# PSUM banks of the decay products, the pool products and the last merge in a two-block transformer kernel

## The chip, the core and the metric

The kernel runs on one core of a Trainium2 chip. Time is device time in microseconds (us) from one launch, which computes everything. TensorE (PE in the rows; PEld is its weight load) does the matrix products and writes them to PSUM, eight banks of 128 partitions x 512 float32. VectorE (DVE) and ScalarE (ACT) read PSUM and work in SBUF; GpSimd (POOL) works in SBUF alone; SyncE (SP) issues the transfers. The order of each engine's instructions is fixed when the program is built; an instruction waits for others by semaphores.

## What is computed

A sequence of 512 tokens of width 1024 goes through two blocks. The first is stick-breaking attention, cross-attention to a memory and a convolutional feed-forward part, each with a layer norm. The change lies in the second block, which takes the normed sequence through one wide projection into three branches and merges them:

```python
w = -softplus(-(w0 + tanh(wd) @ w_up)) - 0.5        # branch a: decay
a = sigmoid(a0 + ad @ a_up)                          #           rate
y_a = rwkv7(r, exp(-exp(w)), k, v, a, ...) * silu(z) # 8 heads of 64, a state carried over 512 steps
y_b = b * conv3(c * u) * silu(z)                     # branch b
pooled[g] = mean over the last 2, 4, 8, 16 tokens of u - u       # branch c
y_c = (einsum('bsgc,gcd->bsgd', pooled, pool_w) * pool_scale) * silu(z)
proj = einsum('nbsc,ncd->nbsd', stack([y_a, y_b, y_c]), w_branch)
merged = sum over n of sigmoid(p_gate[n]) * proj[n]
x = x + rms_norm(merged @ w_out, post_norm_w)
```

## The kernel before

Every large product is done in three passes of single-pass float32 matmuls. Each operand is split into a rounded part and a remainder (`wh`, `wl` for weights; names ending in `h` and `l` for activations), and high x high, high x low and low x high are summed in one bank (`mm3`, L214). The split costs a ScalarE cast and a VectorE subtraction for each weight tile (L144, L145) and each activation tile (L236 and L237, or L1461 and L1462). Activations are kept transposed, with channels on partitions, so a product fills one bank of 128 x 512.

A stream of foreground code issues the projections one after the other: `chunk` takes a bank, runs 24 matmuls into it and hands it to whoever reads it. Background work is written as Python generators that yield a number of ticks; after each 1550 ns of matmul time, by the program's own count, `tick` advances each of them and puts its instructions behind those already issued. That sets the order by hand: nothing is reordered later, and a matmul that waits holds up all that stand behind it on TensorE.

PSUM is given out by `bank`, in four groups of equal tiles, of which each is a ring:

```python
def bank(tag, name, shape=None):
    return psp.tile(shape or [P, S], F32, tag=tag, bufs={"g": 3, "a": 2, "b": 2, "c": 1}[tag], name=name)
```

A product that takes a bank waits until the last reader of the product that had it before is done. Group "g" is used by the projections (`ps_chunk`), the merges (`ps_br`) and the last projection (`ps_rows`); "b" by most small products of the recurrence; "a" by its masked products `ps_ac`, by `ps_w` and by `ps_y`.

The recurrence of branch a runs in the background, for two pairs of heads at a time (`rwkv_pair`). For a pair p it issues: two decay products `ps_wa` (L1040), whose sigmoids `sg` and `ai` ScalarE reads out; the running sum `cs` (VectorE, L1045); the norms `ps_ss` with `ss` and a chain of small VectorE instructions (L1051, L274 to L285), and ScalarE's `rb`; the products `ps_ri` and `ps_rk` (L1066, L1078), the second of which VectorE reads into `bv` (L1080); transposes `ps_tok` (L1098); the masked products `ps_ac` in two halves (L1111), which VectorE reads with L1115 into `aa` and `arr`; then more `ps_tok`, which ScalarE copies into `at` and `kbt` (L1127, L1133).

Meanwhile the foreground issues the projections of branch c. `pool_window` builds the means on GpSimd and VectorE and splits them into `plh` (ScalarE) and `pll` (GpSimd); `pool_mix` multiplies them by `pool_w` into `ps_mix` (three matmuls), which VectorE reads at L1372. The last `merge` (n = 0) makes eight products `ps_br` of 12 matmuls. VectorE multiplies each by its gate (L1401), GpSimd adds it to `merged` (L1402), and `fin`, two products later, splits the sum into `mgh` (ScalarE) and `mgl` (VectorE, L1462). The last projection then reads these in `ps_rows`; its weights are split in the same stretch, the last of them by the L145 that stands at 1312 us.

Of the kernel before, what the change touches and what calls it, by code (L numbers as in the profile page):

```python
# [14 lines left out]
ALU = mybir.AluOpType  # L15
# [53 lines left out]
def model_kernel(ctx: ExitStack, tc: tile.TileContext, a: dict, out: bass.AP, dbg: dict):  # L69
    nc = tc.nc  # L70
    stop = dbg.get("stop")
    V, G, A, T = nc.vector, nc.gpsimd, nc.scalar, nc.tensor
# [14 lines left out]
    def bank(tag, name, shape=None):  # L87
        return psp.tile(shape or [P, S], F32, tag=tag, bufs={"g": 3, "a": 2, "b": 2, "c": 1}[tag], name=name)

    def bigt(name, shape, dt=F32R):  # L90
        return big.tile(shape, dt, tag="B", bufs=5, name=name)
# [4 lines left out]
    def sub(s, *idx):  # L96
        return Split(s.hi[idx], s.lo[idx])
# [52 lines left out]
    def w_take():  # L150
        i = taken[0]
        taken[0] += 1
        while i not in ready:
            w_load()
            if not w_conv():
                assert i in ready, "no room for the weights"
        return ready.pop(i)

    def w_done(n=1):
        freed[0] += n  # L160
# [60 lines left out]
    def mm3(ps, pairs, start=True, stop=True, ticks=True):  # L221

        n = len(pairs)
        for z in range(3):
            for j, (l, r) in enumerate(pairs):
                due = mm(ps, (l.hi, l.hi, l.lo)[z], (r.hi, r.lo, r.hi)[z], start=start and z == 0 and j == 0,
                         stop=stop and z == 2 and j == n - 1)
                if due and ticks:
                    tick()
# [15 lines left out]
    def chunk(x, n=S, tag="g"):  # L245
        ps = bank(tag, "ps_chunk")
        gemm_T(ps[:, 0:n], w_take(), x, 0, n)
        w_done()
        return ps
# [42 lines left out]
    def col(name, j=0, n=1):  # L292
        o = COLS[name] + j
        return colp[:, o:o + n]
# [309 lines left out]
    for c in range(KC):  # L604
        ps = chunk(memT, M)
# [144 lines left out]
    for n in range(2):  # L750
# [8 lines left out]
        for m in range(2):  # L759
            d = (ALLS, m, slice(n * 512, (n + 1) * 512))  # L760
# [56 lines left out]
    for c in range(KC):  # L817
        ps = chunk(hT)
# [71 lines left out]
    for pi, (f0, f1) in enumerate(parts):  # L890
        if pi:
            run_ahead(spare_in(bigt("wxh", [P, 8, 512]), bigt("wxl", [P, 8, 512])))
        for f in range(f0, f1):
# [4 lines left out]
            for isv in range(2):  # L898
                ps = lead.pop(0)() if lead else chunk(hT)
# [79 lines left out]
    def temp(name, shape=None, dt=F32):  # L979
        return b2.tile(shape or [P, S], dt, tag="e", bufs=6, name=name)  # L980
# [52 lines left out]
    def rwkv_pair(p, ab, abd, a21):  # L1033
# [2 lines left out]
        q = p % NB2  # L1036
        sg, ai = slot("sg"), slot("ai")
        for z, (o, b) in enumerate(((sg, "w0"), (ai, "a0"))):
            ps = bank("b", "ps_wa")
            T.matmul(ps, wup[hrow(z), tok(p)], wa[hrow(z)], start=True, stop=True)  # L1040
            A.activation(o, ps, AF.Sigmoid, bias=col(b, p))
        sq = slot("sq")
# [4 lines left out]
        ps = bank("b", "ps_ss")  # L1047
# [16 lines left out]
        ps = bank("b", "ps_ri")  # L1064
# [11 lines left out]
        ps = bank("b", "ps_rk")  # L1076
# [18 lines left out]
        def tokens(src):  # L1095
            ps = bank("b", "ps_tok", [P, 4, P])
            for t in range(NT):
                T.transpose(ps[:, t], src[:, tok(t)], ident)  # L1098
            return ps

        ps = tokens(v)
# [28 lines left out]
        for h in range(2):  # L1130
            ps = tokens(kbh.rearrange("p t z i -> p (t z i)")[:, 512 * h:512 * h + 512])
# [3 lines left out]
        ps = bank("c", "ps_av", [P, NT, 2, CH])  # L1135
# [178 lines left out]
    def y_split(i, x):  # L1314
        yield wait["ysp"]
        split_to(x, ycur["t"][:, 0, i], ycur["t"][:, 1, i], V)
        ysplit.add(i)
# [48 lines left out]
    def pool_mix(i, pw, pooled, zs):  # L1366
        while not pooled:
            yield
        yield wait["mx"]
        ps = bank("b", "ps_mix")  # L1370
        mm3(ps, [(sub(pw, ALLS, i), pooled["h"])], ticks=False)
        V.scalar_tensor_tensor(zs, ps, col("pool_scale", i), zs, ALU.mult, ALU.mult)  # L1372
        yield from y_split(i, zs)

    def gate(g):
        A.activation(g, proj_in(), AF.Sigmoid)
        return g

    def merge(n):
        if "t" not in mT:  # L1380
            mT["t"] = bigt("merged", [P, KC, S], F32)
        merged = mT["t"]
        y = [sub(Split(ycur["t"][:, 0], ycur["t"][:, 1]), ALLS, i) for i in range(4)] if n else ya
        ahead_g = [gate(temp("gate"))] if n else []
        for d in range(KC):
            if n and d < KC - 1:
                ahead_g.append(gate(temp("gate")))
            g = ahead_g.pop(0) if n else gates[:, d]
            if d % 2 == 0:
                w = w_take()  # L1390
            wv = Split(*[x.rearrange("p (c k n) -> p c k n", c=2, k=4) for x in (w.hi, w.lo)])
            if n:
                until(lambda: len(ysplit) == 4)
            ps = bank("g", "ps_br")
            mm3(ps, [(sub(wv, ALLS, d % 2, k), y[k]) for k in range(4)])
            if d % 2:
                w_done()
            if n == 1:
                V.tensor_tensor(merged[:, d], ps, g, ALU.mult)
            else:  # L1400
                V.tensor_tensor(g, ps, g, ALU.mult)  # L1401
                (V if n else G).tensor_tensor(merged[:, d], merged[:, d], g, ALU.add)  # L1402
            if n == 0 and d > 1:
                fin(d - 2)
        if n == 0:
            fin(KC - 2)
            fin(KC - 1)
# [3 lines left out]
    ps = proj_in()  # L1411
# [166 lines left out]
```

## Time and profile before

| | us |
|---|---|
| median of three runs | 1358.63 (1357.41 to 1358.8) |
| the profiled execution | 1359.82 |
| its span, first to last instruction | 1358.1 |
| TensorE busy | 1328.8 |
| VectorE busy | 827.8 |
| ScalarE busy | 527.9 |
| GpSimd busy | 257.4 |

The mean granted clock of TensorE over the span is 0.993. A row of the timeline gives the start, the time to the end of the last of its instructions, engine, line, operation, output and inputs, shape and count, and in brackets how long the engine was idle before it and what ended that. Matmuls overlap, so a row's time is a little longer than the distance to the next start. Where the clock is halved, matmuls take twice as long.

### The profile page before, as it was taken

The page shows a single profiled execution, that of the slowest core. Times are in us where ns is not written, and L with a number is a line of the kernel's source. Part 1 is how long each engine was busy: PE and PEld are TensorE (multiplying, and loading weights), DVE is VectorE, ACT ScalarE, POOL GpSimd, SP SyncE. Part 2 cuts the span into 40 slices and gives each one's busy share as a digit, 9 for nine tenths or more (in the row PEclk, how much of TensorE's full clock was granted, in tenths as well). Part 3 has the DMA queues.
Part 4 walks back from the last instruction along what each step waited for, and adds up shares of the span by engine and source line. Part 5 has one row for each costly group of instructions (what it writes and reads, how often), then busy time and mean ns, then how long its engine had stood idle before and what let it go on. Part 6 is the DMA issues. An engine that isn't in the chain of part 4 may idle for free.

```text
span 1358.1 us, 19442 instructions
## 1 busy us (share of the span) xinstructions
PE 1328.8 (98%) x7804; PEld 1112.2 (82%) x7804; DVE 827.8 (61%) x1425; ACT 527.9 (39%) x780; POOL 257.4 (19%) x244
## 2 busy tenths in 40 slices
PE   8999999999999999999999999999999989999997
PEld 7988888788879888888888888888878768887876
DVE  5787887765577555522556866666335567743575
ACT  6565665144423444321344235532323434222330
POOL 1333432000000434400132211200001342000230
PEclk9999999999999999999999999999999899999999
DMA  5121343242223333233234113234221223422331
GB/s 190 63 90 55 105 148 125 85 148 94 82 74 125 111 94 106 93 103 98 94 124 161 50 57 106 77 107 109 78 79 62 70 76 92 114 89 78 117 132 63
DMA packets 54666, 133.25 MB, mean 98 GB/s; under 512 B 19632, under 2 KB 21552, under 8 KB 54576
## 3 DMA queue, kind: packets, MB, share of 16 engines
q1 hardware_dynamic: 54576, 132.01, 30.7%
q8 instruction: 61, 1.00, 0.3%
q14 instruction: 29, 0.24, 0.1%
HBM read 126.48 MB, written 5.24 MB: 97 GB/s over the span
## 4 chain that ended last, share of the span: by engine, by line
PE 83%; DVE 10%; ACT 3%; DMA 2%; issue 1%; POOL 0%; DVEq 0%; SPq 0%; ACTq 0%; POOLq 0%
PE ps_chunk L214 48%; PE ps_rows L214 9%; PE ps_d L214 6%; PE ps_br L214 3%; PE ps_v L214 3%; PE ps_lead L214 3%; DVE wl L145 2%; PE ps_s L488 1%; PE ps_o L542 1%; ACT wh L144 1%; DVE lnt L650 1%; PE ps_t L510 1%; PE ps_z L214 1%; PE ps_o L214 1%; DMA wr<-in_w_xq_dram 1%
## 5 line engine op out<-in xcount | busy, mean ns | idle before, releaser
L145 DVE TENSOR_TENSOR wl<-wr,wh 128x1024 fp32r<-128x1024 f32 x196 | 251.8, 1286 | 144.5 <-ACT wh L144 143.9
L144 ACT CAST wh<-wr 128x1024 fp32r<-128x1024 f32 x196 | 204.9, 1046 | 116.9 <-PE ps_d L214 51.2
L214 PE MATMUL ps_chunk<-h3Th,wh 128*128 128x512 f32 x480 | 126.0, 398 | 0.0
L214 PE MATMUL ps_chunk<-h3Tl,wh 128*128 128x512 f32 x480 | 125.8, 397 | 0.0
L214 PE MATMUL ps_chunk<-h3Th,wl 128*128 128x512 f32 x480 | 124.3, 395 | 0.0
L872 DVE SCALAR_TENSOR_TENSOR c<-ps_chunk,colp,c 128x511 f32<-128x511 f32 x80 | 59.9, 749 | 92.2 <-ACT c L870 90.7
L878 POOL TENSOR_TENSOR c<-c 128x512 f32<-128x512 f32 x21 | 42.5, 2023 | 357.9 <-ACT c L877 209.3
L214 PEld LDWEIGHTS ps_chunk<-h3Th,wh 128*128 128x128 f32 x480 | 90.0, 190 | 21.1 <-issue 2.3
L214 PEld LDWEIGHTS ps_chunk<-h3Tl,wh 128*128 128x128 f32 x480 | 90.0, 190 | 19.8 <-issue 0.8
L214 PEld LDWEIGHTS ps_chunk<-h3Th,wl 128*128 128x128 f32 x480 | 89.6, 189 | 18.9
L214 PE MATMUL ps_chunk<-h2Th,wh 128*128 128x512 f32 x320 | 79.0, 389 | 0.0
L214 PE MATMUL ps_chunk<-h2Tl,wh 128*128 128x512 f32 x320 | 79.0, 389 | 0.0
L214 PE MATMUL ps_chunk<-h2Th,wl 128*128 128x512 f32 x320 | 79.0, 389 | 0.0
L500 POOL TENSOR_TENSOR w<-r 128x511 f32<-128x511 f32 x40 | 58.7, 1468 | 85.4 <-DVE r L498 76.7
L870 ACT ACTIVATE c<-ps_chunk,colp 128x512 f32<-128x512 f32 x40 | 31.1, 779 | 109.7 <-PE ps_chunk L214 109.7
L214 PEld LDWEIGHTS ps_chunk<-h2Th,wl 128*128 128x128 f32 x320 | 60.1, 188 | 12.5
L214 PEld LDWEIGHTS ps_chunk<-h2Tl,wh 128*128 128x128 f32 x320 | 60.1, 188 | 12.5
L214 PEld LDWEIGHTS ps_chunk<-h2Th,wh 128*128 128x128 f32 x320 | 60.0, 188 | 12.4
L498 DVE TENSOR_TENSOR_SCAN r<-keep,masks 128x512 f32<-128x512 f32 x40 | 59.8, 1509 | 12.5 <-ACT keep L496 8.0
L214 PE MATMUL ps_chunk<-xTh,wh 128*128 128x512 f32 x128 | 35.6, 402 | 5.3 <-ACT xTh L376 5.3
L214 PE MATMUL ps_d<-wh,gvb 128*128 128x512 f32 x128 | 39.7, 389 | 0.0
L496 ACT ACTIVATE keep<-ps_s 128x512 f32<-128x512 f32 (+1 forms) x48 | 24.5, 526 | 37.8 <-PE ps_s L488 37.7
(396 smaller groups left out, 2623.6 us busy)
## 6 DMA issues: line engine op xcount, KB each, us to landing
wr<-in_w_in_dram SPq DMA_DIRECT2D x65, 512.0 KB, 3.6
wr<-in_w_ff_dram SPq DMA_DIRECT2D x44, 512.0 KB, 3.6
wr<-in_w_dn_dram SPq DMA_DIRECT2D x22, 512.0 KB, 3.5
wr<-in_w_qk_dram SPq DMA_DIRECT2D x14, 512.0 KB, 3.5
wr<-in_w_br_dram SPq DMA_DIRECT2D x12, 512.0 KB, 3.5
wr<-in_w_v_dram SPq DMA_DIRECT2D x8, 512.0 KB, 3.7
wr<-in_w_xk_dram SPq DMA_DIRECT2D x8, 512.0 KB, 4.0
wr<-in_w_o_dram SPq DMA_DIRECT2D x8, 512.0 KB, 3.5
```

Source lines behind the costliest of these rows:

```text
L144: A.copy(w.hi, raw)
L145: lo_of.tensor_tensor(w.lo, raw, f32(w.hi), ALU.subtract)
L214: T.matmul(ps, l, r, start=start, stop=stop)
L488: T.matmul(ps[:, o:o + n], q[e][:, tok(i)], part[:, 0:n], start=z == 0 and o == 0, stop=z == 1 and i == parts[-1][1])
L496: A.activation(keep[:, j * n:(j + 1) * n], ps[:, 0:n], AF.Sigmoid, scale=-0.125)
L498: V.tensor_tensor_scan(r[:, ::-1], keep[:, ::-1], masks[:, m, ::-1], 1.0, ALU.mult, ALU.max)
L500: G.tensor_tensor(t[:, 0:S - 1], r[:, 1:S], r[:, 0:S - 1], ALU.subtract)
L510: T.transpose(ps[:, n], src[:, o + j * P:o + (j + 1) * P], ident)
L542: T.matmul(ps[:, j * P:S], lhs, part, start=(j == 0 and z == 0), stop=j == 2 and z == 1)
L870: A.activation(c, ps, AF.Identity, scale=cw(2), bias=col("ffb", j))
L872: V.scalar_tensor_tensor(c[:, 2 - r:S], ps[:, 0:S - 2 + r], cw(r), c[:, 2 - r:S], ALU.mult, ALU.add)
L878: (V if end else G).tensor_tensor(cv, cg, cv, ALU.mult)
```

## The change

It gives three kinds of products other groups of banks, and moves three sums to another engine. The decay products `ps_wa` of pairs 1, 2 and 3 take a bank of group "a"; pair 0 stays on "b". The pool products `ps_mix` take a bank of "g". In the last merge the eight products take their banks from "g", "a" and "b" in turn, so that all seven banks of these groups are used. The sums of its last three products (d = 5, 6, 7) are done by VectorE. Nothing is computed differently.

```diff
@@ rwkv_pair
-            ps = bank("b", "ps_wa")
+            ps = bank("a" if p else "b", "ps_wa")
             T.matmul(ps, wup[hrow(z), tok(p)], wa[hrow(z)], start=True, stop=True)
@@ pool_mix
-        ps = bank("b", "ps_mix")
+        ps = bank("g", "ps_mix")
@@ merge
-            ps = bank("g", "ps_br")
+            ps = bank("g" if n else "gab"[d % 3], "ps_br")
...
-                (V if n else G).tensor_tensor(merged[:, d], merged[:, d], g, ALU.add)
+                (V if n or d > 4 else G).tensor_tensor(merged[:, d], merged[:, d], g, ALU.add)
```

TensorE's instructions stand in the same order as before; what changes is what they wait for. The first place is on TensorE at pair 3's decay products. In brackets stands whose semaphore an instruction waits for (the engine's name).

```order
 L1078 MATMUL ps_rk<-rkh,bd1r 128x512 [waits PE_49,Activation_49]
 L1078 MATMUL ps_rk<-rkl,bd1r 128x512 [waits DVE_49]
-L1040 MATMUL ps_wa<-wa,wup 128x512 [waits PE_49]
-L1040 MATMUL ps_wa<-wa,wup 128x512 [waits DVE_49]
+L1040 MATMUL ps_wa<-wa,wup 128x512 x2
 L214 MATMUL ps_chunk<-h3Th,wh 128x512 x5
 L214 MATMUL ps_chunk<-h3Tl,wh 128x512 x8
 L214 MATMUL ps_chunk<-h3Th,wl 128x512 x3
-L1049 MATMUL ps_ss<-bd_81,sq 128x2 [waits Activation_49]
+L1049 MATMUL ps_ss<-bd_81,sq 128x2 [waits PE_49,Activation_49]
```

The second decay product no longer waits for VectorE; `ps_ss` waits for ScalarE as before.

The second place is on TensorE behind the first pool product, where the transposes `ps_tok` of the scaled keys `kbh` stand between chunk matmuls.

```order
 L214 MATMUL ps_mix<-plh,pw 128x512
 L214 MATMUL ps_chunk<-h3Th,wl 128x512 x5
+L1098 MATMUL ps_tok<-ident,kbh 128x128 [waits Activation_49]
+L1098 MATMUL ps_tok<-ident,kbh 128x128 x3
+L214 MATMUL ps_chunk<-h3Th,wh 128x512 [waits DVE_49]
+L214 MATMUL ps_chunk<-h3Th,wh 128x512 x7
+L214 MATMUL ps_chunk<-h3Tl,wh 128x512 x8
 L1098 MATMUL ps_tok<-ident,kbh 128x128 [waits DVE_49]
 L1098 MATMUL ps_tok<-ident,kbh 128x128 x3
-L214 MATMUL ps_chunk<-h3Th,wh 128x512 x8
-L214 MATMUL ps_chunk<-h3Tl,wh 128x512 x8
-L1098 MATMUL ps_tok<-ident,kbh 128x128 [waits Activation_49]
```

No instruction has moved: the first `ps_tok`, which waited for VectorE, now waits for ScalarE, and the second the other way round. The three `ps_mix` matmuls themselves wait for ScalarE and, the second, for GpSimd in both kernels.

The third place is on VectorE in the last merge, products 4 to 7. `gates` is the gated product, `mgl` the remainder of a sum, `wl` that of a weight tile.

```order
 L1401 TENSOR_TENSOR gates<-ps_br,gates 128x512
+L1402 TENSOR_TENSOR merged<-merged,gates 128x512
 L1462 TENSOR_TENSOR mgl<-merged,mgh 128x512
 L145 TENSOR_TENSOR wl<-wr,wh 128x1024
 L1401 TENSOR_TENSOR gates<-ps_br,gates 128x512
+L1402 TENSOR_TENSOR merged<-merged,gates 128x512
 L1462 TENSOR_TENSOR mgl<-merged,mgh 128x512
 L1401 TENSOR_TENSOR gates<-ps_br,gates 128x512
+L1402 TENSOR_TENSOR merged<-merged,gates 128x512
 L1462 TENSOR_TENSOR mgl<-merged,mgh 128x512 x3
 L145 TENSOR_TENSOR wl<-wr,wh 128x1024
```

Each of the last three gated products is now followed by its sum on VectorE, ahead of the remainders and of the last weight split; GpSimd's row of eight sums has become one of five.

## Rows read from the trace of the kernel before

**Rows 1.** The page's first part: busy time, share of the span, instructions of each engine

```profile
PE 1328.8 (98%) x7804; PEld 1112.2 (82%) x7804; DVE 827.8 (61%) x1425; ACT 527.9 (39%) x780; POOL 257.4 (19%) x244
```

**Rows 2.** TensorE's waits from 1000 us on: total us, times, longest

```profile
PE ps_mix L214 <- ACT at L1127: 3.1, 1, 3.1
PE ps_wa L1040 <- DVE bv L1080: 2.2, 1, 2.2
...
```

**Rows 3.** Timeline of TensorE, 1060 to 1090 us

```profile
1066.23 2.07 PE L1040 MATMUL ps_wa<-wa,wup 64*128 64x512 f32 x2 [2.16 <-DVE bv L1080]
...
1074.22 0.95 PE L1049 MATMUL ps_ss<-bd,sq 128*128 128x2 f32 x8
...
1088.38 1.16 PE L1111 MATMUL ps_ac<-misc,kb 64*128 64x128 f32 x16
...
```

**Rows 4.** Stretches: length, busy us of PE, PEld, DVE, ACT, POOL, granted clock, DMA

```profile
1066.20:1073.00 6.80, 6.77 (x13) 4.29 (x14) 6.33 (x5) 2.61 (x4) 5.30 (x5) 0.50 0.27 78
1100.30:1103.70 3.40, 3.40 (x12) 2.71 (x11) 1.58 (x3) 0.59 (x1) 0.00 (x0) 0.50 0.15 24
1282.00:1298.40 16.40, 16.40 (x73) 13.35 (x72) 11.66 (x12) 9.30 (x11) 6.12 (x3) 1.00 0.71 244
1298.40:1308.00 9.60, 7.79 (x32) 5.77 (x32) 9.60 (x10) 2.81 (x4) 6.04 (x4) 1.00 0.80 259
```

**Rows 5.** Timeline of VectorE, 1055 to 1105 us

```profile
1075.20 0.17 DVE L1051 TENSOR_SCALAR ss<-ps_ss 128x8 f32<-128x8 f32 x1 [2.54 <-PE ps_ss L1049]
...
1087.50 0.41 DVE L1115 TENSOR_TENSOR arr<-ps_ac,tri 128x256 f32<-128x256 f32 x1
...
```

**Rows 6.** Timeline of ScalarE, 1055 to 1120 us

```profile
1098.63 0.59 ACT L1127 COPY at<-ps_tok 128x512 f32<-128x512 f32 x1
```

**Rows 7.** Timeline of GpSimd, 1055 to 1115 us

```profile
1095.90 1.26 POOL L237 TENSOR_TENSOR pll<-ps,plh 128x512 fp32r<-128x512 f32 x1 [1.03 <-ACT plh L236]
...
1111.95 1.27 POOL L237 TENSOR_TENSOR pll<-ps,plh 128x512 fp32r<-128x512 f32 x1 [2.75 <-ACT plh L236]
...
```

**Rows 8.** Timeline of TensorE, 1090 to 1150 us

```profile
1099.27 0.50 PE L214 MATMUL ps_mix<-plh,pw 128*128 128x512 f32 x1 [3.11 <-ACT at L1127]
1099.61 0.39 PE L214 MATMUL ps_mix<-pll,pw 128*128 128x512 f32 x1
...
1101.98 1.05 PE L1098 MATMUL ps_tok<-ident,kbh 128*128 128x128 f32 x4
...
1109.56 2.09 PE L214 MATMUL ps_chunk<-h3Th,wh 128*128 128x512 f32 x8
...
1113.84 0.51 PE L214 MATMUL ps_mix<-plh,pw 128*128 128x512 f32 x1 [1.11 <-ACT kbt L1133]
...
1120.83 1.68 PE L1111 MATMUL ps_ac<-misc,kb 64*128 64x128 f32 x16
...
```

**Rows 9.** Timeline of VectorE, 1104 to 1120 us

```profile
1108.22 0.75 DVE L1372 SCALAR_TENSOR_TENSOR pz_s<-ps_mix,colp,pz_s 128x512 f32<-128x512 f32 x1
```

**Rows 10.** Timeline of TensorE, 1280 us to the end

```profile
1301.85 1.19 PE L214 MATMUL ps_br<-yah,wh 128*128 128x512 f32 x4 [0.38 <-DVE gates L1401]
...
1306.98 0.50 PE L214 MATMUL ps_rows<-wh,mgh 128*128 128x512 f32 x1 [1.43 <-DVE gates L1401]
...
1314.82 0.39 PE L214 MATMUL ps_rows<-wl,mgh 128*128 128x512 f32 x1
...
```

**Rows 11.** Timeline of VectorE, 1294 to 1316 us

```profile
1301.72 0.68 DVE L1462 TENSOR_TENSOR mgl<-merged,mgh 128x512 fp32r<-128x512 f32 x1
...
1302.92 1.18 DVE L1462 TENSOR_TENSOR mgl<-merged,mgh 128x512 fp32r<-128x512 f32 x1
...
1308.05 3.70 DVE L1462 TENSOR_TENSOR mgl<-merged,mgh 128x512 fp32r<-128x512 f32 x3
1312.01 1.23 DVE L145 TENSOR_TENSOR wl<-wr,wh 128x1024 fp32r<-128x1024 f32 x1 [0.25 <-ACT wh L144]
```

**Rows 12.** Line L1402, one form: count, duration in ns min/median/max, first and last start

```profile
L1402 DVE TENSOR_TENSOR merged<-merged,gate x8: 691/692/693, 1161.5 to 1216.1; 128x512 f32<-128x512 f32 x8
```

## Prediction

> **What bounds the kernel now.** I read the page's first part, then the waits of TensorE alone, then the granted clock, then the timelines of the stretches where TensorE stood. The first part says that TensorE is busy for 98% of the span [rows 1]. So an edit pays only where TensorE stands still or runs at half clock, and nearly all of the change lies off that path. In the second half of the program the list of TensorE's waits is short; it is headed by the pool product `ps_mix` and the decay product `ps_wa` [rows 2]. Neither waits for its operands alone. `ps_wa` reads `wa` and `wup`, which are long ready, and was released by VectorE's `bv`, the reader of `ps_rk`, the product that held its bank [rows 3]. The first `ps_mix` was released by ScalarE's `at`, the reader of a `ps_tok`, also on a bank of group "b" [rows 6, 8]. Behind both waits the granted clock shows 0.50: 6.8 us behind the first, 3.4 us behind the second [rows 4], which costs 3.4 and 1.7 us of full-speed work. The last merge has two more waits, 0.38 us in its last product and 1.43 us at the first products of `ps_rows`, both for VectorE's reading of a "g" bank [rows 10]. At stake in all: 2.16 + 3.11 + 1.11 + 0.38 + 1.43 = 8.2 us of standing and 5.1 us of clock. The question is how much comes back as new waits.
>
> **Decay product.** The wait of 2.16 us belongs to pair 3's second `ps_wa` [rows 3]. On group "a" its bank's last reader is done long before, and the listed instructions carry no VectorE wait there any more. TensorE would be 2.16 + 3.4 = 5.6 us ahead by `ps_ss`. What is late next is the second half of `ps_ac`: it needs banks that VectorE's L1115 still reads, until 1087.50 + 0.41 = 1087.91 [rows 5]. VectorE's work up to there started at 1075.20 with `ss`, after 2.54 us of waiting for `ps_ss`; from then on it and ScalarE wait for each other and not for TensorE. Before that wait VectorE was busy, until 1075.20 - 2.54 = 1072.66. With `ps_ss` done early (1074.22 - 5.6 = 1068.6) that chain moves forward by 2.54 us and no more. The second bank of `ps_ac` is then free at 1085.37. It was used 0.2 us after 1088.38, so TensorE leaves `ps_ac` 3.2 us ahead, and 2.4 us have come back as a new wait. The decay products of pairs 1 and 2 had no listed wait: nothing. A wait on group "a" could cost something only if the readers there were late.
>
> **Pool product.** With 3.2 us in hand TensorE reaches the first `ps_mix` at 1099.27 - 3.11 - 3.2 = 1093.0. Now it waits for data. GpSimd's `pll` was done at 1095.90 + 1.26 = 1097.16 [rows 7]; 2.54 us earlier is 1094.62. The second matmul of the product, which reads it, moves from 1099.61 to 1094.62: 5.0 us ahead. The bank of `at` now goes to the next `ps_tok`, five chunk matmuls on. `at` ends at 1098.63 + 0.59 = 1099.22, and 2.54 earlier is 1096.68, against the 1101.98 of before: **5.3 us** ahead [rows 6, 8]. That number does not hang on the clock between the two products, since TensorE waits for the chain there anyway. Behind it, 1.7 us of the half-clock stretch (1101.98 to 1103.70) are left, worth **0.9** if the clock stays up. If it falls behind the new waits instead, a stretch like that of before costs 1.7, that is 2.6 less than I take. The second `ps_mix` waited 1.11 us for `kbt`. `pll` was ready at 1111.95 + 1.27 = 1113.22; TensorE without its wait would read it at 1113.84 - 1.11 + 0.34 = 1113.07 (0.34 from the first product's two starts), so 0.2 stay and **0.9** are won. The second half of the next `ps_ac` took 1.68 us where its sibling took 1.16 [rows 3, 8]; VectorE, which no longer trails, should free that bank sooner: 0 to 0.5, I take **0.4**. The third and fourth products show no wait. The product now holds one of three "g" banks until VectorE's L1372 ends, at 1108.22 + 0.75 = 1108.97, and the second chunk after it starts at 1109.56 [rows 8, 9]: 0.6 us to spare, and both move with the same `ps_tok` between them. A VectorE instruction stretched by 0.5 us [rows 11] would still fit. I take nothing, at most 0.3.
>
> **Last merge.** With seven banks no product waits for the reading three products back, and the first two `ps_rows` get banks that were read long before: 0.38 + 1.43 = **1.8 us**. Behind this is the last weight split of VectorE, ending at 1312.01 + 1.23 = 1313.24, needed by the matmul that stood at 1314.82; without its waits TensorE comes at 1313.0. The three sums cost VectorE 0.69 us each [rows 12], 2.1 us ahead of that split. Against it: the remainder `mgl` takes 0.68 us when GpSimd is still and 1.18 and 3.70/3 = 1.23 when it adds [rows 11]. Four of them get 0.5 us shorter, and the 0.25 us of idle goes, so the split ends between 1312.9 and 1313.1, just in time. If the remainders kept their length it would end at 1315.1 and TensorE would wait 2.1 us, which takes the whole gain of the merge; I take the first, since GpSimd has nothing else to do there.
>
> The Trainium skill ("SBUF — State Buffer", section "Who interferes with whom") says that a VectorE instruction with two inputs in SBUF contends with a GpSimd instruction that reads SBUF. By that rule the split ends at 1312.9, by its absence at 1315.1; this trace agrees with it, 0.68 against 1.18 us [rows 11].
>
> **Sum.** 5.3 + 0.9 + 0.9 + 0.4 + 1.8 = 9.3 us, against 8.2 + 5.1 at stake. The profiled execution took 1359.82 us (span 1358.1), so 1350.5. The median of the runs is 1358.63, 1.2 us lower, and 1349.3 by the same sum. If those runs ran 1.2 us less at half clock, the sum is as much smaller for them and the result is 1350.5 again. I take **1350.0 us**.
>
> **The rivals.** (1) *The clock falls behind the new waits.* For: the new wait at `ps_ac` is 2.4 us and those at `ps_mix` and `ps_tok` together 1.6 to 1.9, and waits of 2.16 and 3.11 us were followed by half clock. Against: the 1.43 us were not [rows 4], and what is lost between `ps_ac` and `ps_mix` is hidden by the next wait. Cost: 2.6 us behind `ps_tok`, 1.7 more if a stretch of 6.8 us starts at `ps_ac`: 1352.6, up to 1354.3. (2) *The chain of VectorE and ScalarE doesn't start earlier*, because `ss` has another late input. Then only the second pool product and the merge pay, 0.9 + 1.8 = 2.7 us: 1356. Against: VectorE's wait names `ps_ss` [rows 5]. (3) *The edit doesn't change the waits*, because the banks handed out have readers as late as before: 1358.6. Against: the waits in the listing of the change. (4) *Slower, by the clock.* The new waits follow closely, at about 1083, 1093 and 1096 us, and between them the clock doesn't come back. Standing shrinks by 8.2 us and grows by about 4.5 in new waits (2.4 + 1.7 + 0.4), 3.7 net, so with H us of half clock in all the time is 1358.6 - 3.7 - 5.1 + H/2: slower from H = 17.6, where before showed 10.2. Half clock from there through to where the second `ps_mix` stood, 1113.84, would be some 28 us, and 1364. Against: the clock came back after 3.4 and 6.8 us, and in the longer stretch TensorE was at work for 6.77 of 6.80 us [rows 4].
>
> The Trainium skill ("TensorE: Matmul & The Clock Gate", section "A second HAM failure mode: psum-queue depth-cycling") tells of a kernel that cycled through PSUM banks, paused briefly between groups and lost throughput to a clock that kept falling and rising. That rule speaks for (4), in the merge too, which now cycles through three groups. This trace does not bear it out: the merge of before cycles through three banks and shows clock 1.00 in both of its stretches [rows 4].
>
> **How the numbers follow.** Forecast 0.70 (own range 1348.3 to 1352), rival (1) 0.18, (2) 0.06, (3) 0.04, (4) 0.02. The range reaches from 1347.8 (the clock never falls, and the waits counted from the starts of the matmuls, which is some tenths more at each) to rival (1)'s 1354.0; that leaves out (2) to (4) and a rest of the others. A difference of 0.2%, 2.7 us, is about what can be told from none. Faster by more: forecast, (1), and half of (2), 0.91. Same: the rest of (2) and (3), 0.07. Slower: (4), 0.02.
>
> **What would show it.** No idle at `ps_wa`; a wait of some 2.4 us at the second half of `ps_ac`, released by L1115; idle at `ps_mix` of 1 to 2 us in all, released by `plh` or `pll`, and a short one at the `ps_tok` behind it, released by `at`; none at `ps_br` and the first `ps_rows`; `mgl` of 0.7 us after the fifth product; VectorE's idle at `ss` gone. The forecast is wrong if VectorE still waits for `ps_ss`, if the half-clock stretches add up to over 7 us behind 1096, or if the last weight split holds `ps_rows` for over 0.5 us.

## The result, and the profile after

The changed kernel takes 1350.24 us, beside 1358.02 for the kernel before. That is the median of four executions: 1349.22, 1349.54, 1350.93, and one of 1498.88 us with a mean clock of 0.824, which the ratio leaves out. The ratio is 0.9941, 95% interval [0.9927, 0.9955]: 8.0 us less, and the interval does not hold 1. 1350.0 was predicted, with a range of 1347.8 to 1354.0. The profiled execution took 1349.54 us, 10.3 less than the one of before.

The page's first part: span, then busy time, share and instructions of each engine. Of TensorE's busy time 6.2 us are gone [rows 1]; what bounds the kernel is the same.

```profile
span 1347.8 us, 19442 instructions
...
PE 1322.6 (98%) x7804; PEld 1108.6 (82%) x7804; DVE 833.7 (62%) x1428; ACT 527.2 (39%) x780; POOL 248.1 (18%) x241
```

TensorE's waits from 1000 us on (total us, times, longest), the whole list. The two that headed the list of before [rows 2] are gone, and one new one stands there.

```profile
PE ps_ac L1111 <- DVE arr L1115: 3.6, 2, 3.4
PE ps_yT L1302 <- POOL misc L1297: 0.3, 1, 0.3
```

The timeline of TensorE from there, as in [rows 3, 8]: no idle time at `ps_wa`, 3.41 us at the second half of `ps_ac`, and none in brackets at the two `ps_mix`, at the `ps_tok` between them and at the second half of the next `ps_ac` (1.16 us where it took 1.68).

```profile
1061.86 1.13 PE L1040 MATMUL ps_wa<-wa,wup 64*128 64x512 f32 x4
...
1084.39 0.46 PE L1111 MATMUL ps_ac<-misc,kb 64*128 64x128 f32 x2 [3.41 <-DVE arr L1115]
1085.05 1.74 PE L1111 MATMUL ps_ac<-misc,kb 64*128 64x128 f32 x14 [0.20 <-DVE arr L1115]
...
1094.42 0.40 PE L214 MATMUL ps_mix<-pll,pw 128*128 128x512 f32 x1
...
1096.28 0.66 PE L1098 MATMUL ps_tok<-ident,kbh 128*128 128x128 f32 x4
...
1106.80 0.50 PE L214 MATMUL ps_mix<-pll,pw 128*128 128x512 f32 x1
...
1113.55 1.16 PE L1111 MATMUL ps_ac<-misc,kb 64*128 64x128 f32 x16
```

Stretches with the granted clock (length, busy us of PE, PEld, DVE, ACT, POOL, clock, DMA). Before had three stretches of half clock between 700 us and the last matmul, 13.6 us in all; this execution has one, 3.4 us, right behind the new wait. In the last merge the clock is up.

```profile
1085.40:1088.80 3.40, 3.40 (x18) 2.79 (x16) 2.71 (x4) 0.62 (x1) 3.24 (x4) 0.50 0.67 237
1088.80:1110.00 21.20, 20.99 (x135) 16.55 (x135) 14.23 (x23) 9.04 (x15) 11.60 (x12) 1.00 0.21 51
1290.00:1300.00 10.00, 10.00 (x46) 8.29 (x45) 9.93 (x14) 3.25 (x5) 3.33 (x2) 1.00 0.79 259
```

The timeline of TensorE in the last merge: the rows follow each other at 0.91 us, and `ps_rows` begins without a wait [rows 10].

```profile
1295.08 1.07 PE L214 MATMUL ps_br<-yah,wl 128*128 128x512 f32 x4
1295.99 0.39 PE L214 MATMUL ps_rows<-wh,mgh 128*128 128x512 f32 x1
```

VectorE there [rows 11]: the added sums (L1402) take 1.07 and 0.69 us, the remainders `mgl` 0.68, the last three 1.89 in place of 3.70, and the last weight split follows without idle time.

```profile
1295.35 1.07 DVE L1402 TENSOR_TENSOR merged<-merged,gates 128x512 f32<-128x512 f32 x1
1296.33 0.68 DVE L1462 TENSOR_TENSOR mgl<-merged,mgh 128x512 fp32r<-128x512 f32 x1
...
1298.78 0.69 DVE L1402 TENSOR_TENSOR merged<-merged,gates 128x512 f32<-128x512 f32 x1
...
1301.32 1.89 DVE L1462 TENSOR_TENSOR mgl<-merged,mgh 128x512 fp32r<-128x512 f32 x3
1303.13 1.22 DVE L145 TENSOR_TENSOR wl<-wr,wh 128x1024 fp32r<-128x1024 f32 x1
```

**Where the time went.** The same matmul in two timelines shows how far TensorE is ahead. Four of them are used below, by their start in before: the first `ps_wa` of pair 3 (1062.95), one in the second half of the next `ps_ac` (1121.38), the first matmuls of the last merge's sixth product (1292.94), the last `ps_rows` (1349.72). At the first of them after is already 1.1 us ahead. That arose in the first 310 us, where nothing was changed; in the other kernels that keep the order it is from -0.1 to 1.3, so it is what two executions differ by. From the first to the second ("the stretch") 6.5 us are won, to the third 0.2, from there to the last ("the merge") 2.45: 9.2 us. The ratio shows 1.2 us less than that. The two profiles differ by more than the edit: in before a load came 1.0 us later (last section). By estimate that is 1.0 us of the stretch, if each us of the load is one there. The profiled execution of before was also among those with most half clock, and that of after, at 0.998, had the least of its kernel. Beside the experiments, the thirteen executions of before with a mean clock of 0.993 or 0.994 took 1357.7 to 1360.0 us, the four with 0.999 took 1354.9 to 1357.4.

### The profile page after: what moved, and what is told of

It is laid out like the page before. It is cut to its first block, busy times and chain, and to the rows that moved or that the text cites. A ratio compares the mean times of both kernels' runs of the same rounds, so it can differ in the third digit from the quotient of the medians.

```text
span 1347.8 us, 19442 instructions
## 1 busy us (share of the span) xinstructions
PE 1322.6 (98%) x7804; PEld 1108.6 (82%) x7804; DVE 833.7 (62%) x1428; ACT 527.2 (39%) x780; POOL 248.1 (18%) x241
## 4 chain that ended last, share of the span: by engine, by line
PE 85%; DVE 9%; ACT 3%; issue 1%; DMA 1%; POOL 0%; DVEq 0%; SPq 0%; ACTq 0%; POOLq 0%
PE ps_chunk L214 48%; PE ps_rows L214 9%; PE ps_d L214 6%; PE ps_br L214 5%; PE ps_v L214 4%; PE ps_lead L214 3%; DVE wl L145 2%; PE ps_s L488 1%; PE ps_o L542 1%; DVE lnt L650 1%; PE ps_t L510 1%; PE ps_z L214 1%; PE ps_o L214 1%; DVE rs_t L279 1%; PE ps_w L1214 1%
## 5 line engine op out<-in xcount | busy, mean ns | idle before, releaser
L145 DVE TENSOR_TENSOR wl<-wr,wh 128x1024 fp32r<-128x1024 f32 x196 | 255.6, 1305 | 141.2 <-ACT wh L144 140.5
```

The costliest lines, as they stand in the source:

```text
L145: lo_of.tensor_tensor(w.lo, raw, f32(w.hi), ALU.subtract)
```

## Experiments

The theory: from `ps_ss` on, VectorE and ScalarE work through one chain, which feeds `ps_ac`, `ps_mix` and `ps_tok` in turn; TensorE's waits there are waits for that chain, so that one taken away comes back at the next product. The first rival: each wait is worth what it showed, and gains add up. The second, against which the last runs stand: VectorE is the bound there in any order.

| kernel | median us | ratio to before, 95% | ahead at 1062.95 | won in the stretch | won in the merge |
|---|---|---|---|---|---|
| after | 1350.24 | 0.9941 [0.9927, 0.9955] | 1.1 | 6.5 | 2.45 |
| after_again | 1349.87 | 0.9944 [0.9931, 0.9958] | 1.0 | 5.45 | 2.6 |
| decay_only | 1356.65 | 0.9984 [0.9975, 0.9993] | -0.1 | 3.5 | -0.15 |
| pool_only | 1353.61 | 0.9964 [0.9952, 0.9977] | 0.3 | 5.6 | 0.0 |
| decay_pool | 1354.72 | 0.9969 [0.9957, 0.9980] | 0.8 | 5.2 | -0.1 |
| merge_only | 1356.48 | 0.9985 [0.9976, 0.9993] | -0.1 | 0.4 | 2.6 |
| sums_back | 1352.34 | 0.9961 [0.9949, 0.9974] | 0.0 | 5.9 | 1.4 |
| banks_back | 1353.56 | 0.9970 [0.9958, 0.9981] | 1.3 | 4.7 | 0.1 |
| ac_banks | 1351.67 | 0.9952 [0.9939, 0.9964] | 0.3 | 5.9 | 2.5 |
| p4_ac_banks | 1350.04 | 0.9942 [0.9929, 0.9954] | another order | | |
| spread_a | 1350.45 | 0.9950 [0.9937, 0.9962] | another order | | |
| spread_cg | 1346.22 | 0.9920 [0.9908, 0.9933] | another order | | |
| spread_cg_mp | 1344.88 | 0.9910 [0.9897, 0.9924] | another order | | |

The medians of before beside them were 1359.10 (the first four experiments), 1358.23 (the next four) and 1357.33 (the last four, after_again among them). An execution of before lay between 1354.88 and 1360.90, so differences of 1 us between two rows say little; the last three columns come from one profile of each.

### decay_only: the decay products alone

```diff
-            ps = bank("b", "ps_wa")
+            ps = bank("a" if p else "b", "ps_wa")
```

> Before, with the decay products of pairs 1 to 3 in group a, and nothing else changed. Theory (one chain through VectorE and ScalarE): the 2.16 us wait of ps_wa goes, and with it the 6.8 us of half clock behind it (3.4 lost), so TensorE is 5.6 ahead; 2.4 to 3.4 of that comes back as a wait of the second half of ps_ac for arr (L1115), and the first ps_mix, still in group b, waits again for at, which moves only by VectorE's 2.54 idle at ss. Sum: 2.6 us less (1.0 to 3.5), ratio 0.998. Rival (each wait is gained where it stood): 2.16 + 3.4 = 5.6 us less, ratio 0.996, and no new wait.

TensorE's waits from 1000 us on:

```profile
PE ps_ac L1111 <- DVE arr L1115: 3.4, 1, 3.4
...
PE ps_mix L214 <- ACT kbt L1133: 1.1, 1, 1.1
PE ps_mix L214 <- ACT at L1127: 0.5, 1, 0.5
```

As the theory has it: the wait of `ps_wa` is gone and stands at `ps_ac`, with 6.8 us of half clock behind it that eat most of the wait that `ps_mix` had. The ratio means 0.9 to 3.4 us less, against 2.6 by the theory and 5.6 by the rival, which falls.

### pool_only: the pool products alone

```diff
-        ps = bank("b", "ps_mix")
+        ps = bank("g", "ps_mix")
```

> Before, with the pool products in group g, and nothing else changed. Theory (one chain): the wait of ps_wa for bv and the half clock behind it stay as in before; the first ps_mix waits 0.5 to 1.5 for plh and pll in place of 3.11 for at, ps_tok 0.4 for at, the second ps_mix 0.3 in place of 1.11: 3.3 us less (2.5 to 4.5), ratio 0.9975. Rival (each wait is gained where it stood): 3.1 + 1.1 = 4.2 less, and together with the decay product alone 9.8. What tells them apart is the sum over the two single runs and the run with both.

Waits of TensorE, then VectorE's row of `ss`:

```profile
PE ps_wa L1040 <- DVE bv L1080: 1.8, 1, 1.8
...
PE ps_mix L214 <- POOL pll L237: 0.8, 1, 0.8
...
PE ps_tok L1098 <- ACT at L1127: 0.2, 1, 0.2
```

```profile
1072.92 0.17 DVE L1051 TENSOR_SCALAR ss<-ps_ss 128x8 f32<-128x8 f32 x1 [0.98 <-PE ps_ss L1049]
```

The waits are where the theory put them, but the gain is larger, 4.9 us by the ratio (3.1 to 6.5) and 5.6 in the stretch against 3.3. The ratio's interval still holds the theory's 3.3, and the rival's 4.2 as well; this run alone does not tell them apart. Two things differ from the profile of before, both ahead of the first `ps_mix` and so not the edit's: `ps_wa` waits 1.8 us instead of 2.16 and half clock behind it lasts 3.4 us, not 6.8. So VectorE waits 0.98 us for `ps_ss`, not 2.54, and its chain runs 1 us ahead of that in before. The merge_only kernel, which leaves this stretch as it was, shows the same there (1.36 us of wait, 3.4 of half clock). The profile of before had the longer of two forms of this stretch.

### decay_pool: both together

The two edits above.

> Before, with the decay products of pairs 1 to 3 in a and the pool products in g; the last merge as before. Theory (one chain): 5.9 to 6.7 us less (ratio 0.9954), of which the decay product's own share on top of the pool products is 2.6 to 3.3, about what the half clock behind ps_wa lost and no more. ps_ac's second half waits 2.4 to 3.6 for arr. Rival (gains add up): 5.6 + 4.2 = 9.8 us less, ratio 0.993.

TensorE's longest wait of its second half:

```profile
PE ps_ac L1111 <- DVE arr L1115: 4.3, 1, 4.3
```

The rival's 9.8 us are out: the ratio means 2.7 to 5.8. But so is the theory's range, 5.9 to 6.7, if only just: a miss. With both edits the kernel is no faster than with the pool products alone, by the medians (1354.72 and 1353.61) and by the stretch (5.2 and 5.6). What the decay product spares comes back at `ps_ac`, all of it as far as these runs can tell, with 6.8 us of half clock behind it, where pool_only has 3.4 behind `ps_wa`.

### merge_only: the last merge alone

```diff
-            ps = bank("g", "ps_br")
+            ps = bank("g" if n else "gab"[d % 3], "ps_br")
-                (V if n else G).tensor_tensor(merged[:, d], merged[:, d], g, ALU.add)
+                (V if n or d > 4 else G).tensor_tensor(merged[:, d], merged[:, d], g, ALU.add)
```

> Before, with the last merge's banks from three groups and its last three sums on VectorE; decay and pool products as before. Theory: the waits 0.38 (ps_br) and 1.43 (first ps_rows) go and the last weight split comes just in time: 1.8 to 2.5 us less, ratio 0.9984. Rival: the split of the last weight on VectorE, queued behind the three added sums, holds ps_rows 2.1: 0.2 less or more, ratio 1.000. If the parts are independent, this run and the one with decay and pool products together come to the whole change, 7.8 us of the medians.

2.0 us by the ratio (0.9 to 3.3), 2.6 in the profile, and no wait in the merge. Nothing here speaks against the parts being independent: the ratios of decay_pool and this run together take off 0.46% (0.31 and 0.15), the whole change 0.59 and 0.56%, within what the intervals leave open.

### sums_back: the sums on GpSimd again

```diff
-                (V if n or d > 4 else G).tensor_tensor(merged[:, d], merged[:, d], g, ALU.add)
+                (V if n else G).tensor_tensor(merged[:, d], merged[:, d], g, ALU.add)
```

> After, with the last three sums of the last merge back on GpSimd (banks as in after). Theory: GpSimd's adds (1.7 to 2.2 us each) read beside VectorE's products, mgl takes 1.2 in place of 0.68, and the split of the last weight ends 0.7 to 2.1 too late for ps_rows: 0.7 to 2.1 us more than after, so 5.7 to 7.1 less than before, ratio 0.9953. Rival: the sums on VectorE cost as much as the contention that they spare, and the banks alone carry the gain of the merge: as after, ratio 0.994.

VectorE's rows of the remainders and the last split, then TensorE's row:

```profile
1301.91 3.70 DVE L1462 TENSOR_TENSOR mgl<-merged,mgh 128x512 fp32r<-128x512 f32 x3
1305.87 1.23 DVE L145 TENSOR_TENSOR wl<-wr,wh 128x1024 fp32r<-128x1024 f32 x1 [0.26 <-ACT wh L144]
```

```profile
1307.15 0.50 PE L214 MATMUL ps_rows<-wl,mgh 128*128 128x512 f32 x1 [0.77 <-DVE wl L145]
```

The three remainders take 3.70 us again, as in before, the split is late, and TensorE waits 0.77 for it: 1.1 us less is won in the merge than with the sums on VectorE. That is at the lower end of the theory's 0.7 to 2.1. It rests on the rows: the ratio, 0.9961 beside 0.9941 and 0.9944, is too wide to tell it from none.

### banks_back: the merge in group "g" again

```diff
-            ps = bank("g" if n else "gab"[d % 3], "ps_br")
+            ps = bank("g", "ps_br")
```

> After, with the last merge's products back in group g alone (the last three sums stay on VectorE). Theory: ps_br waits 0.2 to 0.7 for the eviction again, and the first ps_rows 1.2 to 2.3, since VectorE now has three adds ahead of the eviction that frees its bank: 1.8 to 2.9 us more than after, 5.0 to 6.0 less than before, ratio 0.996. Rival: the banks only mattered because of slow sums on GpSimd, so that with the sums on VectorE nothing waits: as after, ratio 0.994.

TensorE's waits:

```profile
PE ps_rows L214 <- DVE gates L1401: 1.0, 1, 1.0
PE ps_br L214 <- DVE gates L1401: 0.7, 2, 0.4
```

The waits are back, the one at `ps_rows` a little under the 1.2 to 2.3 expected. With three banks the sums on VectorE alone win nothing: 0.1 us in the merge, 2.4 less than after, as the theory had it (1.8 to 2.9). So of the 2.5 us the banks alone give 1.4 (sums_back), the sums alone 0.1, and the rest comes from both.

### ac_banks: the new wait taken away

```diff
-            pss = [bank("a", "ps_ac", [P, 4, 2, CH]) for _ in range(2)]
+            pss = [bank("cg"[e] if o else "a", "ps_ac", [P, 4, 2, CH]) for e in range(2)]
```

> After, with the second half of ps_ac in groups c and g, so that it need not wait for the evictions of the first half. Theory (one chain): the 3.4 us wait at ps_ac becomes 0 to 1.3, and TensorE waits as long a little later, at ps_mix behind the same evictions (2 to 3.6) or at ps_tok for at: no change against after within 0.4 us, ratio 0.994 to before. Rival (TensorE's waits are bank waits that can be taken away one by one): 2.1 to 3.4 us less than after, ratio 0.992.

TensorE's row of the first pool product:

```profile
1093.80 0.48 PE L214 MATMUL ps_mix<-plh,pw 128*128 128x512 f32 x1 [3.38 <-DVE arr L1115]
```

The wait of 3.4 us has gone from `ps_ac` to `ps_mix`, nearly unchanged in size and with the same releaser, and nothing is won: 5.9 us in the stretch, ratio 0.9952. The edit has put half of that `ps_ac` into group "g", where `ps_mix` takes its bank, so one could think that the wait is this ring's alone. It isn't: the second matmul of the product reads `pll`, which GpSimd ends in the same trace at 1094.38, so TensorE, there since 1090.42, would have stood nearly as long for data. In after `pll` ends at 1094.17 and that matmul starts at 1094.42.

```profile
1093.11 1.27 POOL L237 TENSOR_TENSOR pll<-ps,plh 128x512 fp32r<-128x512 f32 x1 [1.02 <-ACT plh L236]
1094.43 0.80 PE L214 MATMUL ps_mix<-pll,pw 128*128 128x512 f32 x1 [0.16 <-POOL pll L237]
```

This is the plainest run for the chain and against waits as something that is taken away one by one.

### p4_ac_banks: the chain's second part called a step earlier

As ac_banks, and one of the numbers of ticks that the background work yields (p4 stands between `ps_rk` and the first `ps_tok`):

```diff
-    "gate": 4, "p1": 2, "p2": 5, "p3": 4, "p4": 4, "ac": 2, "tk": 2, "inv": 1, "invn": 2, "pw0": 4, "pw1": 4,
+    "gate": 4, "p1": 2, "p2": 5, "p3": 4, "p4": 3, "ac": 2, "tk": 2, "inv": 1, "invn": 2, "pw0": 4, "pw1": 4,
```

> The same as the run with ps_ac in groups c and g, and the work of each pair from the value transposes on is called one step earlier (p4 3 for 4), so that TensorE reaches ps_tok and ps_ac with less of the other stream's work behind it and VectorE's chain is fed earlier. Theory (one chain, whose start is what counts): the chain of evictions starts earlier and so does all behind it; 4 to 6 us less than after, 12 to 14 less than before, ratio 0.990. Rival: VectorE is the bound there and its chain only gets the same work in another order: as after, ratio 0.994.

TensorE's row, then the half-clock stretch behind it:

```profile
1080.92 2.07 PE L1111 MATMUL ps_ac<-misc,kb 64*128 64x128 f32 x14 [3.32 <-DVE pz_s L1015]
```

```profile
1080.70:1087.50 6.80, 6.58 (x27) 5.48 (x28) 5.86 (x11) 1.80 (x3) 5.70 (x8) 0.50 0.32 89
```

A miss for the theory as I had put it: nothing is won (0.9942). TensorE comes to a stop at the second half of `ps_ac` 3.4 us earlier than in after (1080.92 - 3.32 against 1084.39 - 3.41, without the idle time). VectorE's chain did not start earlier for it: its last `arr` of the first half stands at 1083.24, 1.25 us ahead of that in after (1084.49), but the cast of the pool weights, on which that chain hangs (last section), also began 1.20 us sooner (1059.25 against 1060.45). And the bank is now held by the reading of a projection (`pz_s`, L1015), which stands in the same chain. Behind this wait no other one follows, and so the 6.8 us of half clock, with TensorE at work for 6.58 of them, are lost in full, 3.3 us; in after the waits that were due at `ps_mix` and `ps_tok` hid a part. After spends 3.6 us of waiting here and 1.7 of clock, a part of it covered; this kernel 3.3 and 3.3.

### after_again, spread_a, spread_cg, spread_cg_mp: the two pairs pulled apart

The odd pair's work starts one step later, and the steps of the inverse behind it are taken three at a time:

```diff
-    "gate": 4, "p1": 2, "p2": 5, "p3": 4, "p4": 4, "ac": 2, "tk": 2, "inv": 1, "invn": 2, "pw0": 4, "pw1": 4,
-    "pw2": 6, "pw3": 7, "mx": 4, "ysp": 1, "gl": 1, "xc": 14, "x1": 1, "x2": 2, "x3": 2, "so": 2, "mp": 2, "pp": 3,
+    "gate": 4, "p1": 2, "p2": 5, "p3": 4, "p4": 4, "ac": 2, "tk": 2, "inv": 1, "invn": 3, "pw0": 4, "pw1": 4,
+    "pw2": 6, "pw3": 7, "mx": 4, "ysp": 1, "gl": 1, "xc": 14, "x1": 1, "x2": 2, "x3": 2, "so": 2, "mp": 2, "pp": 4,
```

spread_a has this alone, spread_cg also the edit of ac_banks, spread_cg_mp also `"mp": 1` in place of 2 (the stages of the chunk maps, one step each). The two numbers of spread_a were changed together, and which of them counts is not shown. after_again is the changed kernel itself.

> The changed kernel itself, beside the three that follow. Theory (the chain through VectorE sets the time from the second half of ps_ac to the second ps_mix): the wait of ps_ac for arr is there with 3 to 4.3 us, the half clock behind it lasts 3.4 or 6.8 us and is mostly taken out of the waits that would follow at ps_mix and ps_tok; ratio 0.994 to 0.996 to before. Rival (the gain rests on which stretches of half clock an execution happens to have): the ratio is not repeated.

> After, with the odd pair's preparation called one projection step later (pp 4 for 3), so that VectorE's work of the two pairs collides less, and the inverse's steps taken three at a time (invn 3 for 2), so that the stage behind is not later; ps_ac as in after. Theory: the second half of ps_ac still waits 3 to 4 us for arr with half clock behind it, but the waits at ps_mix and ps_tok (2 us in all with the clock up) are gone: 0 to 3.5 less than after, depending on how much of the half clock is left uncovered. Rival (the stretch costs the same in any order, as with p4 one step earlier): as after within 0.7.

> The same as the run before, and the second half of ps_ac in groups c and g. Theory: no wait of TensorE in the stretch is longer than 1.1 us, so that the clock stays up, and what after still spends there (3.6 at ps_ac, 1.7 lost to half clock, 0.3 at the second ps_mix) goes: 4 to 7 us less than after, ratio to before 0.990. Rival (VectorE is the bound there and the wait only turns up elsewhere, as in the runs with ps_ac in c and g): as after within 0.7.

> The same as the run before, with the chunk maps' stages called every step (mp 1 for 2), so that the transposes of ps_yT come a step earlier. Theory: as the run before or up to 1 us less, 4 to 8 less than after. Rival: as after within 0.7.

TensorE's waits from 1000 us on, in spread_a:

```profile
PE ps_ac L1111 <- DVE arr L1115: 2.9, 2, 2.7
```

in spread_cg:

```profile
PE ps_chunk L214 <- ACT gate L1376: 1.1, 1, 1.1
...
PE ps_mix L214 <- DVE arr L1115: 0.4, 1, 0.4
```

in spread_cg_mp, with its stretch from 1060 to 1130 us:

```profile
PE ps_mix L214 <- DVE arr L1115: 0.4, 1, 0.4
```

```profile
1060.00:1130.00 70.00, 69.54 (x418) 54.94 (x417) 49.45 (x80) 36.20 (x53) 34.78 (x36) 1.00 0.28 89
```

after_again repeats the result (3.8 us of wait at `ps_ac`, this time with 6.8 us of half clock). spread_a is not faster than it (1350.45 and 1349.87): 2.7 us of wait stay at `ps_ac`, with 3.4 of half clock. There the rival's forecast came true (as after within 0.7); the theory's 0 to 3.5 us less did not show. spread_cg is, by 3.65 us (1346.22), just under the 4 to 7 expected, and spread_cg_mp by 5.0 (1344.88). Neither shows half clock anywhere in this part, and in spread_cg_mp TensorE is at work for 69.54 of 70 us. So the second rival falls too: VectorE was not the bound, it had 20 of those 70 us free. The other banks for `ps_ac` are worth nothing in the order of after and 4 us in the other; the other order is worth nothing without them. spread_cg_mp beats both kernels: 12.2 us less than before by its ratio (10.3 to 14.0).

## Why the prediction was right, step by step

The mechanism was right: one wait taken away came back, smaller, at the next product of the same chain, and the merge lost its waits. The total was right too (9.3 us against 9.2 between the same matmuls), but that it came out to 0.1 us is luck: one term was 0.7 too large and one 0.65 too small, and 1.0 of the 9.2 came with a load that the edit did not touch (last section). The range's upper end, 1354.0, is 0.3 under rival (1)'s own sum of 1354.3; nothing hangs on it. What follows is net of the 1.1 us by which after was ahead before the stretch.

- **Decay product: the new wait at `ps_ac` right in kind, undersized.** The wait was to be 2.4 us and is 3.41 + 0.20. The step that failed is "that chain moves forward by 2.54 us and no more": `arr` is 1087.50 - 1084.49 - 1.1 = 1.9 ahead. The 2.54 us of VectorE's idle at `ss` did vanish, and `ss` itself is 3.5 ahead (the other 1.0 came with a load, last section), but the small instructions behind it take 1.6 us more. The timelines of VectorE and GpSimd in after, below, show why. So the edit itself moved `arr` by only 0.9 us, the rest of the 1.9 is the load. This is the term "5.3 at `ps_tok`", which measured 1101.98 - 1096.28 - 1.1 = 4.6, the load's 1.0 included.

```profile
1070.57 0.15 DVE L1051 TENSOR_SCALAR ss<-ps_ss 128x8 f32<-128x8 f32 x1
1070.75 0.17 DVE L274 TENSOR_SCALAR rs_v<-ss 128x8 f32<-128x8 f32 x1
1070.83 1.01 DVE L275 TENSOR_SCALAR rs_n<-ss 128x8 f32<-128x8 f32 x1
...
1072.16 0.94 DVE L282 TENSOR_TENSOR rs_t<-rs_t,rs_n 128x8 f32<-128x8 f32 x1
...
1073.34 1.24 DVE L281 TENSOR_TENSOR rs_t<-rs_y 128x8 f32<-128x8 f32 x1
```

```profile
1070.77 1.05 POOL L1357 TENSOR_TENSOR ps<-ps 128x510 f32<-128x510 f32 x1
...
1072.04 1.03 POOL L1357 TENSOR_TENSOR ps<-ps 128x508 f32<-128x508 f32 x1
...
1073.29 1.27 POOL L1357 TENSOR_TENSOR ps<-ps 128x504 f32<-128x504 f32 x1
```

  Three instructions of 128 x 8, else 0.15 to 0.17 us, last until the GpSimd sum that began just before them ends: 1071.84 and 1071.82, 1073.10 and 1073.07, 1074.58 and 1074.56. In before two of these sums ran out while VectorE stood idle, and one such collision was left, 1.17 us at L274. VectorE, starting earlier, met all three. The Trainium skill ("SBUF — State Buffer", section "Who interferes with whom") says that where an instruction of VectorE and one of GpSimd contend, the one issued second is blocked until the first has ended; this trace agrees, to 0.03 us. I had weighed that rule in the merge, for `mgl`, and not here.
- **Pool product: right.** `ps_mix` needs no wait for `at` any more. The rest of the half-clock stretch and the second `ps_mix` brought 1.7 more by 1106.80 (1114.18 - 1106.80 - 1.1 = 6.3, less 4.6), against 0.9 + 0.9. The wait for `pll` of "1 to 2 us" that was to show at the first `ps_mix`, and the short one at `ps_tok`, are not there: the half-clock stretch behind `ps_ac` used up that time, as rival (1)'s own text said of what is lost between `ps_ac` and `ps_mix`. The next `ps_ac` brought 0.2 against 0.4.
- **Rival (1), the clock behind the new waits.** It fell behind `ps_ac` in both profiles of the changed kernel, 3.4 and 6.8 us, and stayed up behind `ps_mix`, where no wait was left. The stretch won 6.5 and 5.45 us. Of that difference 0.4 us is a later load (last section), so the longer stretch cost some 0.7 us, less than the 1.7 I gave it; the rest was hidden by waits that were due anyway.
- **The parts' shares: wrong.** I had credited the 3.4 us of clock behind `ps_wa` to the decay product, and in the expectation of decay_pool I gave it 2.6 to 3.3 us on top of the pool products. The runs show no gain on top of them; with the pool products alone the stretch is worth as much.
- **Last merge: right in kind, undersized.** 1.8 us predicted, 2.45 measured. The split of the last weight is in time, with nothing to spare: it ends at 1304.35, and the matmul that needs it starts at 1304.40. The reason given (`mgl` 0.68) is not all of it. The four remainders got 2.3 us shorter and the three sums cost 2.45, the first of them 1.07. What saved it is a term that I had left out: the weight split between the products, which in before stood beside GpSimd's sums (1301.87 to 1305.24), takes 1.1 us less. Its row in before, then in after with the row of TensorE:

```profile
1304.02 2.31 DVE L145 TENSOR_TENSOR wl<-wr,wh 128x1024 fp32r<-128x1024 f32 x1
```

```profile
1296.93 1.21 DVE L145 TENSOR_TENSOR wl<-wr,wh 128x1024 fp32r<-128x1024 f32 x1
1304.40 0.50 PE L214 MATMUL ps_rows<-wl,mgh 128*128 128x512 f32 x1
```

  VectorE shows no idle time in after between this split and the last one, so with 2.31 there the last one would, by estimate, have ended at 1305.45 and held TensorE for 1.05 us. In sums_back both come back, 2.31 for this split and 3.70 for the remainders. The term failed in its unit: I added up idle times, and a stop costs more than its idle time, as I had allowed only in the lower end of the range. The rows of before ahead of the two waits in [rows 10]:

```profile
1300.40 1.07 PE L214 MATMUL ps_br<-yah,wl 128*128 128x512 f32 x4
...
1305.16 0.39 PE L214 MATMUL ps_rows<-wh,mgl 128*128 128x512 f32 x1
```

  From start to start there are 1301.85 - 1300.40 = 1.45 us around the 0.38 us, where after has 0.91, so 0.54 are lost; and 1306.98 - 1305.16 = 1.82 around the 1.43 us, where after has 0.22 to 0.23, so 1.59. The rows overlap when nothing waits (1.07 us long, 0.91 apart), and a wait takes that overlap away too. Smaller losses at and behind the stops make up the rest.
- **Rivals (2) to (4)** are out: VectorE no longer waits for `ps_ss`, the waits did change, and half clock shrank from 13.6 to 3.4 us (6.8 in after_again). The rule of the Trainium skill ("TensorE: Matmul & The Clock Gate", section "A second HAM failure mode: psum-queue depth-cycling") does not show here: the merge now cycles through three groups at clock 1.00, and spread_cg_mp, where `ps_ac` takes banks of two further groups, keeps it too.

## What to carry to other kernels

When a product waits for a bank, look at who reads that bank and what this reader waits for in turn: if several waits hang on one chain, another bank moves the wait to the next product, and only the sum of what the chain allows is won. Take the banks and the order together: here neither showed a gain alone, and together they were worth 4 us; with both, the waits were short and the clock stayed up throughout that part. And count a stop of TensorE by the starts of the rows around it, not by its idle time.

## What the runs showed of the hardware

**The chain hangs on a load.** The one thing that I had not reckoned with: ScalarE's cast of the pool weights `pw_raw` waits for their transfer in all fourteen profiles; SyncE issues it behind two weight tiles, and what ScalarE and VectorE do next stands behind that cast. The rows of ScalarE, first of before, then of after:

```profile
1062.53 0.62 ACT L236 CAST pw<-pw_raw 128x512 fp32r<-128x512 f32 x1 [4.11 <-DMA pw_raw<-in_pool_w_dram]
```

```profile
1060.45 0.62 ACT L236 CAST pw<-pw_raw 128x512 fp32r<-128x512 f32 x1 [3.12 <-DMA pw_raw<-in_pool_w_dram]
```

From the start of this cast to the last `arr` of the first half, which frees TensorE at `ps_ac`, it takes in the seven profiles that keep the order and in which VectorE did not wait for `ps_ss`:

| | cast | last `arr` | between |
|---|---|---|---|
| after | 1060.45 | 1084.49 | 24.04 |
| after_again | 1060.88 | 1084.90 | 24.02 |
| decay_only | 1061.62 | 1085.66 | 24.04 |
| decay_pool | 1061.64 | 1085.65 | 24.01 |
| sums_back | 1062.13 | 1086.16 | 24.03 |
| banks_back | 1060.85 | 1084.87 | 24.02 |
| ac_banks | 1060.68 | 1084.72 | 24.04 |

TensorE's own place moves against the cast in these seven: its first `ps_wa` starts 0.5 to 2.0 us behind it. In before, pool_only and merge_only, where VectorE waits 2.54, 0.98 and 0.96 us for `ps_ss`, it takes 24.97, 24.38 and 24.19, so these waits cost the chain only 0.9, 0.35 and 0.2 us. In p4_ac_banks it takes 23.99, and in the three kernels of the other order 22.27 or 22.28: that order makes the chain itself 1.75 us shorter.

So with the decay products on other banks the time at which `ps_ac` is freed is set by when 256 KB land, 5.3 us after their issue in after and 6.2 in before, and the 2.54 us at `ss` that I built on were a second wait in the same chain. A part of what differs from execution to execution comes from there, the 1.0 us by which the load was later in before among it (1062.53 - 1060.45 - 1.1); counted from TensorE's first `ps_wa`, the load is later in before than in the nine other profiles of that order. That an earlier load would bring more in the order of after is what the table suggests; it was not tried.

**Half clock after the same wait, or not.** At 786 us TensorE waits 2.2 us for `h3Tl` in every one of these profiles. In six of the fourteen (before, pool_only, merge_only, sums_back, ac_banks, p4_ac_banks) 3.4 us of half clock follow, in the others none. It costs nothing there: with the clock up, the next product (`ps_hT`, for the same `h3Tl`) waits 1.2 us in place of 0.3 or less. At the places compared here half clock was paid in full only where no wait stood behind it. Nor was it only the longer waits that it followed: the 1.36 us at `ps_wa` in merge_only were followed by half clock, the 1.43 us in the last merge of before, which I had named against rival (1), were not. What decides whether it follows stays open.
